# One decoder layer in fp32 on one core: merged rows kept on chip for a first operand, the gate's norm moved behind its product, final sums on VectorE, the last rows stored in two unequal parts

## The chip, the core and the metric

The kernel runs on one NeuronCore of a Trainium2 chip. The core has five engines, each with its own instruction queue that is worked off in order: TensorE (PE, matrix products into PSUM), VectorE (DVE, elementwise), ScalarE (ACT, elementwise with a function, a scale and a running sum), GpSimd (POOL) and SyncE (SP, which here issues all DMA transfers). Engines wait for each other through semaphores. The metric is the device time of one execution in microseconds (us); less is better. The time before is the median of three runs, 1106.02 us (1105.62 to 1108.62).

## The reference

One layer on x of shape (1024, 1024), all in fp32, cut to what matters here:

```python
h = rms_norm(x, norm_mix_g)
q, k, v, z_a, gk_low, cb, cc, xc, z_c, g_a, g_c = split(h @ w_in)
o = rms_norm(gla_chunked(q, k, v, gk), gla_norm_g)
y_a = (o * silu(z_a)) @ w_branch_a
y_c = ((cb * causal_dwconv(cc * xc, conv_w)) * silu(z_c)) @ w_branch_c
merged = sigmoid(g_a + b_ga) * y_a + sigmoid(g_c + b_gc) * y_c
x = x + merged @ w_out
ple_gate = sigmoid(rms_norm(x, norm_ple_g) @ w_ple_gate)
x = x + ple_gate * (p @ w_ple_proj)
return rms_norm(x, norm_final_g)

def rms_norm(x, g):
    return x * rsqrt(mean(x * x) + EPS) * g
```

The places of the change are `merged @ w_out`, the gate `rms_norm(x) @ w_ple_gate` and the last two lines.

## The kernel before

**Products.** Each fp32 product is made of three passes over a high and a low part of both operands (`mm3`; `split` makes the high part on ACT and the low part on DVE). A block product of 1024 x 1024 operands is made by a scheme with seven sub-products of 512 x 512 pieces in place of eight (`Cell.run`, products 0 to 6). An operand has four quadrants, loaded as raw tiles 0 to 3 (tag `raw`, eight buffers), and three to four sums of them: S1 = raw 1 + raw 3, S2 = S1 - raw 0, S3 and S4. A cell's products gather in three PSUM banks X, V and Y. Product 1 needs S1; V is copied or added out after product 1, and product 5 goes on in V. Cells run in pairs, their products alternating in the order 0, 1, 2, 3, 5, 4, 6. `run_groups` makes the operands (`prep`) up to seven products ahead and the loads up to thirteen.

**Stages.** Projections of h (`v`, `za`, `q`/`k`), the convolution branch (`conv`), gates, with the attention woven in (`att`), then the branch products `yc0..3` and `ya0..3`, the output projection `out0..3`, and the gate `gt0..3`. Of the last two, cell p holds the row blocks 2p and 2p + 1 (128 rows each). `merge_a` adds the two branches into a tile `ga`, which goes to the DRAM array `md`; `out` cells load their raw tiles from `md`.

**Around the output projection.** `make_out` loads two row blocks of x of 128 x 1024 into tiles of the pool `late`, which takes the place of the pool `sw`. The product is added onto them; the left halves by `cons`, the right halves straight from the banks Y and V by `onto`. A squared sum of each half gives the norm factor r (`rstd_of`, two POOL operations, the second a power of -0.5). `flip` scales the rows by r on ACT, turns them by PE transposes of 128 x 128 and multiplies them by the gain `gple` on DVE into tiles `gr` (three buffers), which go to the DRAM array `gd`, from where `gt` cells load. The rows themselves go to the DRAM array `x2d` once both halves are added.

**Around the end.** `make_gate` gives sigmoid on ACT, two DVE operations (times the projected embedding `pe`, plus x), a square with a sum on ACT, and the closing norm. The row blocks i = 1 of cells 2 and 3 are closed in pieces (`piece`): a block's pieces each add a sum (`pre`, `rf`; POOL), and the last piece makes the factor. Cell 3's last product is made in two halves of 256 columns, so that block has three pieces: columns 512 to 1023, 0 to 255, 256 to 511.

**Order.** The program is noted first and put in order by a planner (`Flow`): each operation has a cost, a latency and a due time counted back from the end; `put_in_order` lets the engine that can start first start the most urgent operation that is ready by then. PE's products keep the program's order; transposes (`side`) go where they fit. Buffers of a tag are given out in the order in which the program uses them first, so a tile that waits for a buffer holds back later tiles of its tag. `weave` spreads a generator's steps over the products: the weights of `w_out` and `w_ple_gate` (w = 0 and 1) are combined in the conv phase by `weights`, from tiles `wt` in place, and go to the DRAM arrays `wtd`; `bq` names the arrays that a stage loads.

All noted operations are issued by one line (491 in the profile), so groups are told apart by the names of their tiles.

Of the kernel before, what the change touches and what calls it, by code (L numbers as in the profile page):

```python
# [16 lines left out]
P = 128  # L17
# [229 lines left out]
class Flow:  # L247
# [12 lines left out]
    def note(self, engine, op, call, args, kw):  # L260
# [14 lines left out]
        o.lat = 0.15  # L275
        if engine == PE:
# [226 lines left out]
def kernel(  # L503
# [70 lines left out]
    gd = [[dram(f"gd{p}_{q}", 2, 4, P) for q in range(2)] for p in range(4)]  # L574
    wtd = [[dram(f"wtd{w}_{n}", 4, 512) for n in range(4)] for w in range(2)]

# [85 lines left out]

    def ring_steps(name, side, raw):

# [16 lines left out]
        if side == "A":  # L681
            a11, a21, a12, a22 = (r(n) for n in range(4))
            return [lambda: put(a11()), lambda: two("S1", a21, a22, ALU.add), lambda: two("S2", k("S1"), a11),
                    lambda: put(a12()), lambda: two("S3", a11, a21), lambda: two("S4", a12, k("S2"), over="S2"),
                    lambda: put(a22())]
# [9 lines left out]
    class Cell:  # L695


        def __init__(self, name, side, src, res, cons, prods=ORDER, begin=None, s1=None, u2=None, s5=None):
# [5 lines left out]
            self.steps = ring_steps(name, side, self.raw)  # L704

        def load(self, k):
            for n in NEED[self.side][k]:
                if self.raw[n] is None:
                    self.raw[n] = bp.tile([P, 4, P], F32, tag="raw", name=f"{self.name}raw{n}", bufs=8)
                    load(self.raw[n], self.src[n])  # L710
# [114 lines left out]

    def rstd_of(ms, name, ms2=None, tag="rstd"):
        r = sm.tile([P, 1], F32, tag=tag, name=name, bufs=4)
        if ms2 is None:
# [116 lines left out]

    merged = set()

    def merge_a(c, pool):
        def cons(i, j, src):
# [26 lines left out]
    nc.side = False  # L976
    for n in range(9):
        mm(warm[n % 6], zero[:, 0:P], zero, start=True, stop=True)
# [546 lines left out]
    def bq(w):  # L1525
        return [wb[w, 0], wtd[w][0], wtd[w][1], wb[w, 3], wtd[w][2], wb[w, 2], wtd[w][3]]

# [13 lines left out]
    for p in range(4):  # L1541
        outs.append(Cell(f"out{p}", "A", [md[p // 2][:, p % 2, n // 2, n % 2] for n in range(4)], wres, None))
    for c in outs[:2]:
# [5 lines left out]
    with phase("late", [ph["sw"], ep]) as lp:  # L1549
        flipped = set()  # L1550

        def make_out(p, cell):
# [3 lines left out]
            def begin():  # L1556
                for i in range(2):
                    xt.append(lp.tile([P, D], F32, tag="x", name=f"x2_{p}_{i}", bufs=4))
                    load(xt[i], x[rows(2 * p + i), :])
                    ms.append(sm.tile([P, 2], F32, tag="ms2", name=f"ms2_{p}_{i}", bufs=4))  # L1560

            def flip(i, r):
                act(xt[i], xt[i], AF.Copy, scale=r[:, 0:1])
                yield 4
                for qq in range(2):
                    pt = pso.tile([P, 4, P], F32, tag="o", name=f"pt_g{p}_{i}_{qq}", bufs=2)
                    for k in range(4):
                        kk = 4 * qq + k
                        transpose(pt[:, k, :], xt[i][:, kk * P:(kk + 1) * P])
                    g = lp.tile([P, 4, P], F32, tag="gr", name=f"gr{p}_{i}_{qq}", bufs=3)  # L1570
                    tt(g, pt, gple[:, 4 * qq:4 * qq + 4, None].to_broadcast([P, 4, P]), op=ALU.mult)
                    store(gd[p][qq][:, i], g)
                    yield 1
                flipped.add((p, i))

            def finish(i, j):
                js = slice(j * 512, (j + 1) * 512)
                act(junk[:, 0:512], xt[i][:, js], AF.Square, scale=1.0 / 32.0, accum_out=ms[i][:, j:j + 1])
                seen[i] += 1
                if seen[i] == 2:  # L1580
                    store(x2d[2 * p + i], xt[i])
                    r = rstd_of(ms[i][:, 0:1], f"rg{p}_{i}", ms[i][:, 1:2], tag="rg")
                    weave(flip(i, r), 4)

            def onto(i):
                def add(src):
                    tt(xt[i][:, 512:], src, xt[i][:, 512:], op=ALU.add)
                    return xt[i][:, 512:]
                return add

            def cons(i, j, src):
                if j == 0:
                    tt(xt[i][:, 0:512], src, xt[i][:, 0:512], op=ALU.add)
                finish(i, j)
# [7 lines left out]
        for p, c in enumerate(gts):  # L1602
            c.ready = lambda k, p=p: {(p, 0), (p, 1)} <= flipped
        with phase("sw4", lp.instead, lp) as pool:
# [4 lines left out]
        with phase("fin", [ph["sw4"]], lp) as gp:  # L1609
# [3 lines left out]
            def make_gate(p, cell):  # L1613
# [5 lines left out]
                def piece(i, cs, src, n, done):  # L1619
# [26 lines left out]
                    if a:  # L1646
                        nc.vector.tensor_scalar(xt[i][:, 0:a], xt[i][:, 0:a], r[:, 0:1], None, op0=ALU.mult)
                    store(out[rows(2 * p + i), 0:512], xt[i][:, 0:512])
# [15 lines left out]
                def cons(i, j, src):  # L1664
# [6 lines left out]
                    load(t, ped[2 * p + i][:, js])  # L1671
                    act(src, src, AF.Sigmoid)
                    tt(t, src, t, op=ALU.mult)
# [82 lines left out]
```

## Time and profile before

| What | us |
|---|---|
| median of three runs | 1106.02 |
| runs, lowest to highest | 1105.62 to 1108.62 |
| the profiled execution | 1105.2 |
| its span, first to last instruction | 1103.1 |
| PE busy | 1090.3 |
| DVE busy | 864.9 |
| ACT busy | 588.2 |
| POOL busy | 60.9 |

The profile is of one execution, whose time is 2.1 us over its span. Rows of a timeline give start, duration, engine, line, operation, output <- inputs and shapes; a bracket tells how long the engine was idle ahead of it and who ended that. Matmuls are pipelined: each is shown with some 0.39 us, while neighbours of 512 columns start 0.23 us apart, so a short stall shows in the starts and not in the busy time. `SPq` rows are DMA issues, and their duration is that of the issue, not of the transfer. Rows that group instructions give the count, then busy time and mean ns. Rows of stretches give the stretch and its length, then busy time and count of PE, weight loads, DVE, ACT and POOL, the granted PE clock, the share of the DMA engines and GB/s.

### The profile page before, as it was taken

How to read it: one execution, taken by the hardware profiler on the slowest of the kernel's cores; microseconds unless marked ns; L12 is line 12 of the kernel's file. 1: busy time of each engine (PE TensorE's matmuls, PEld its weight loads, DVE VectorE, ACT ScalarE, POOL GpSimd, SP SyncE). 2: the span in 40 equal slices, each digit the busy share in tenths (PEclk: the TensorE clock that was granted, in tenths of full speed). 3: DMA queues.
4: the chain of work that ended last, by engine and by line, in shares of the span. 5: the costliest groups of instructions: out<-in, count | busy, mean ns of one | idle time of the engine just before them, and what ended most of it. 6: DMA issues, size and time to landing. Idle time of an engine off the chain costs nothing. (4 is left out here: it accounts for less than half of the span.)

```text
span 1103.1 us, 15242 instructions
## 1 busy us (share of the span) xinstructions
PE 1090.3 (99%) x5049; PEld 907.2 (82%) x5049; DVE 864.9 (78%) x1391; ACT 588.2 (53%) x1083; POOL 60.9 (6%) x121
## 2 busy tenths in 40 slices
PE   9999999999999999999999999999999999999996
PEld 7888888788888888888888888888888887788885
DVE  6996477889878887748649687776999879879676
ACT  6775347866543433343334376765736344558554
POOL 0000000000000000000000022220000000102022
PEclk9999999999999999999999999999999999999998
DMA  9957463358777582212212699987694878788853
GB/s 317 326 188 241 135 211 106 115 186 249 243 228 259 170 290 99 89 58 67 86 63 74 224 302 350 324 259 278 237 306 158 307 260 296 273 271 297 293 182 133
DMA packets 149118, 235.79 MB, mean 214 GB/s; under 512 B 12592, under 2 KB 66096, under 8 KB 145968
## 3 DMA queue, kind: packets, MB, share of 16 engines
q1 hardware_dynamic: 149040, 234.83, 63.5%
q8 instruction: 39, 0.64, 0.2%
q14 instruction: 39, 0.32, 0.1%
HBM read 157.19 MB, written 77.59 MB: 213 GB/s over the span
## 5 line engine op out<-in xcount | busy, mean ns | idle before, releaser
L491 ACT ACTIVATE junk<-x 128x512 bf16<-128x512 f32 (+1 forms) x33 | 20.3, 617 | 20.4 <-DVE x L491 20.0
L491 ACT ACT_TABLE_LOAD x17 | 21.8, 1283 | 3.4 <-issue 2.4
L491 POOL MEMSET t<- 128x2 f32 x8 | 0.8, 99 | 378.4 <-DVE u L491 194.8
L491 DVE TENSOR_TENSOR wt<-wt 128x512 f32<-128x512 f32 x32 | 21.4, 684 | 0.2
L491 POOL TENSOR_TENSOR or<-or,mhalf 128x1 f32<-128x1 f32 x32 | 20.4, 639 | 2.7
L491 POOL TENSOR_SCALAR rg<-ms 128x1 f32<-128x1 f32 x8 | 5.9, 736 | 265.4 <-ACT junk L491 265.4
L491 DVE SCALAR_TENSOR_TENSOR u<-t,vec,u 128x1024 f32<-128x1024 f32 x16 | 20.4, 1276 | 0.0
L491 DVE COPY_PREDICATED aT<-trim,X 128x128 f32<-128x128 int32 x32 | 9.7, 302 | 13.3 <-PE X L491 12.7
L491 ACT ACTIVATE og<-op,or 128x256 f32<-128x256 f32 x32 | 15.1, 472 | 9.0 <-POOL or L491 7.4
L491 ACT CAST aTh<-aT 128x128 fp32r<-128x128 f32 x32 | 9.5, 298 | 11.3 <-DVE aT L491 9.9
L491 POOL TENSOR_SCALAR or<-oms 128x1 f32<-128x1 f32 x32 | 8.8, 275 | 118.9 <-ACT junk L491 118.9
L491 PE MATMUL op<-vl,aTh 128*128 128x256 f32 x64 | 15.0, 316 | 0.0
L491 PE MATMUL op<-Sh,qkl 128*128 128x256 f32 x56 | 14.5, 281 | 0.0
L491 DVE TENSOR_TENSOR gr<-pt_g,vec 128x512 f32<-128x512 f32 x16 | 10.7, 685 | 4.4 <-PE pt_g L491 3.6
L491 DVE TENSOR_TENSOR oT<-op,szl 128x256 f32<-128x256 f32 x32 | 13.3, 420 | 0.8 <-DMA szl<-szd 0.6
L491 ACT ACTIVATE junk<-op 128x256 bf16<-128x256 f32 x32 | 12.3, 385 | 2.0 <-PE op L491 1.7
L491 DVE TENSOR_TENSOR Sl<-S,Sh 128x256 fp32r<-128x256 f32 x28 | 11.8, 421 | 1.4 <-ACT Sh L491 1.1
L491 PE MATMUL pe<-wpehi,pThi 128*128 128x512 f32 x32 | 12.8, 399 | 0.0
L491 PE MATMUL pe<-wpehi,pTlo 128*128 128x512 f32 x32 | 12.7, 397 | 0.0
L491 PE MATMUL pe<-wpelo,pThi 128*128 128x512 f32 x32 | 12.6, 393 | 0.0
L491 PEld LDWEIGHTS X<-vl,keh 128*128 128x128 f32 x56 | 10.5, 188 | 2.3
L491 PE MATMUL X<-qkl 128*128 128x128 f32 x64 | 12.3, 274 | 0.0
(3231 smaller groups left out, 4158.1 us busy)
## 6 DMA issues: line engine op xcount, KB each, us to landing
qkl<-qkd SPq DMA_DIRECT2D x32, 320.0 KB, 4.8
wt<-in_wb_dram SPq DMA_DIRECT2D x8, 1024.0 KB, 6.4
wtd<-wt SPq DMA_DIRECT2D x32, 256.0 KB, 3.5
vl<-vd SPq DMA_DIRECT2D x32, 256.0 KB, 4.7
vraw<-in_wb_dram SPq DMA_DIRECT2D x28, 256.0 KB, 4.2
uq<-ud SPq DMA_DIRECT2D x5, 1024.0 KB, 6.4
oq<-od SPq DMA_DIRECT2D x5, 1024.0 KB, 6.0
hq<-in_xT_dram SPq DMA_DIRECT2D x8, 512.0 KB, 8.0
```

The source lines that it names most:

```text
L491: o.call(*[place(a) for a in o.args], **{k: place(a) for k, a in o.kw.items()})
```

## The change

- **Merged rows on chip.** For the row half i = 0 and the column blocks 4 to 7, `merge_a` writes the sum into a tile of the tag `raw` (`late`, named m4 to m7). It is still stored to `md`. `out0` and `out1` form S1 from raw tile 1 and these tiles, in four additions of 128 x 128 (`fresh`); raw tile 3 is loaded later, for product 6.
- **The norm in the gate's sigmoid.** The gain `gple` is multiplied into the weights of `w_ple_gate` on ACT in `weights` (16 operations of 128 x 512), and the three scaled quadrants go to three more arrays of `wtd` (12 stores). The rows are turned unscaled, half by half as soon as a half is added; a copy on ACT takes them out of PSUM. The factor r comes in as the scale of the gate's sigmoid (`rgate`).
- **x by halves.** For cells 0 and 1 the right halves of x are loaded into buffers of the tags `u2` and `s5`; `x2d` is stored by halves.
- **Sums by DVE.** The small additions of `piece` move from POOL to DVE; the power stays on POOL.
- **The last rows.** The closing scale of the last block is split into columns 640 to 1023 (ACT, stored by a DMA that ACT issues) and 0 to 639 (DVE, stored through SP); the last piece's product with the closing gain becomes an operation of its own ahead of the factor. For the block i = 1 of cell 2 the right half's scale moves from DVE to ACT.
- **Warm-up.** Ten matmuls in place of nine at the start; the planner knows a cost for a DMA issued by ACT.

```diff
@@ ring_steps
+            def s1():
+                if not fresh:
+                    return two("S1", a21, a22, ALU.add)
+                t = keep["S1"] = bp.tile([P, 4, P], F32, tag="T", name=f"{name}S1", bufs=4)
+                for kt in range(4):
+                    tt(t[:, kt, :], a21()[:, kt, :], fresh[kt](), op=ALU.add)
+                return put(t)
@@ merge_a
-            tt(g, g, m, op=ALU.add)
+            if i == 0 and k >= 4:
+                t = late[k - 4] = bp.tile([P, 512], F32, tag="raw", name=f"m{k}", bufs=8)
+                tt(t, g, m, op=ALU.add)
+                g = t
+            else:
+                tt(g, g, m, op=ALU.add)
@@
-    for n in range(9):
+    for n in range(10):
         mm(warm[n % 6], zero[:, 0:P], zero, start=True, stop=True)
@@ weights
+                    if w:
+                        for n, q in enumerate((b11, b12, b22, b21)):
+                            k = kt + 4 * (n >= 2)
+                            act(q, q, AF.Copy, scale=gple[:, k:k + 1])
+                            if n != 1:
+                                store(wtd[w][4 + (n + 1) // 2][:, kt, :], q)
@@ make_out
+                    t = lp.tile([P, D], F32, tag="x", name=f"x2_{p}_{i}", bufs=4)
+                    xt.append([t[:, 0:512], t[:, 512:]])
+                    if p < 2:
+                        xt[i][1] = bp.tile([P, 512], F32, tag=("u2", "s5")[i], name=f"x2r{p}_{i}", bufs=2)
...
-            def flip(i, r):
-                act(xt[i], xt[i], AF.Copy, scale=r[:, 0:1])
...
-                    tt(g, pt, gple[:, 4 * qq:4 * qq + 4, None].to_broadcast([P, 4, P]), op=ALU.mult)
+            def flip(i, j):
...
+                nc.scalar.copy(g, pt)
@@ finish
+                store(x2d[2 * p + i][:, j * 512:(j + 1) * 512], xt[i][j])
+                weave(flip(i, j), 2)
...
-                    store(x2d[2 * p + i], xt[i])
-                    r = rstd_of(ms[i][:, 0:1], f"rg{p}_{i}", ms[i][:, 1:2], tag="rg")
-                    weave(flip(i, r), 4)
+                    rgate[p, i] = rstd_of(ms[i][:, 0:1], f"rg{p}_{i}", ms[i][:, 1:2], tag="rg", bufs=8)
@@ piece
-                    act(src, src, AF.Sigmoid)
+                    act(src, src, AF.Sigmoid, scale=rgate[p, i][:, 0:1])
...
+                    if a or not done:
+                        tt(xc, xc, gf[:, cs], op=ALU.mult)
                     if not done:
-                        tt(xc, xc, gf[:, cs], op=ALU.mult)
...
-                        nc.gpsimd.tensor_scalar(pre, m, EPS if n == 0 else sums[i][:, 0:1], None, op0=ALU.add)
+                        nc.vector.tensor_scalar(pre, m, EPS if n == 0 else sums[i][:, 0:1], None, op0=ALU.add)
...
-                    nc.gpsimd.tensor_scalar(r, m, sums[i][:, 0:1], None, op0=ALU.add)
+                    nc.vector.tensor_scalar(r, m, sums[i][:, 0:1], None, op0=ALU.add)
                     nc.gpsimd.tensor_tensor(r, r, mhalf, op=ALU.pow)
                     if a:
-                        act(xt[i][:, 512:], xt[i][:, 512:], AF.Copy, scale=r[:, 0:1])
-                    else:
-                        nc.vector.tensor_scalar(xt[i][:, 512:], xt[i][:, 512:], r[:, 0:1], None, op0=ALU.mult)
+                        part = xt[i][:, 640:]
+                        act(part, part, AF.Copy, scale=r[:, 0:1])
+                        nc.scalar.dma_start(out[rows(2 * p + i), 640:], part)
+                        part = xt[i][:, 0:640]
+                        nc.vector.tensor_scalar(part, part, r[:, 0:1], None, op0=ALU.mult)
+                        store(out[rows(2 * p + i), 0:640], part)
+                        return
+                    act(xt[i][:, 512:], xt[i][:, 512:], AF.Copy, scale=r[:, 0:1])
```

More of the change, by code (lines that the diff above doesn't have):

```diff
@@ L275, in note @@
         o.lat = 0.15
-        if engine == PE:
+        if engine == ACT and op == "dma_start":
+            o.cost, o.lat = 0.1, 3.0
+        elif engine == PE:
             o.cost, o.lat = n / 2400 + 0.0134, 0.22
@@ L574 @@
     gd = [[dram(f"gd{p}_{q}", 2, 4, P) for q in range(2)] for p in range(4)]
-    wtd = [[dram(f"wtd{w}_{n}", 4, 512) for n in range(4)] for w in range(2)]
+    wtd = [[dram(f"wtd{w}_{n}", 4, 512) for n in range(4 + 3 * w)] for w in range(2)]
     load = nc.sync.dma_start
@@ L661, with ring_steps @@
             "B": ((0,), (0, 1), (2,), (3,), (2, 1), (2,), (3,))}
-    def ring_steps(name, side, raw):
+    def ring_steps(name, side, raw, fresh):
         keep = {}
@@ L682, in ring_steps @@
             a11, a21, a12, a22 = (r(n) for n in range(4))
-            return [lambda: put(a11()), lambda: two("S1", a21, a22, ALU.add), lambda: two("S2", k("S1"), a11),
+            def s1():
[5 more added lines that the diff above has]
+                return put(t)
+            return [lambda: put(a11()), s1, lambda: two("S2", k("S1"), a11),
                     lambda: put(a12()), lambda: two("S3", a11, a21), lambda: two("S4", a12, k("S2"), over="S2"),
@@ L703, in __init__ @@
             self.raw, self.ring = [None] * 4, {}
-            self.steps = ring_steps(name, side, self.raw)
+            self.steps, self.fresh = ring_steps(name, side, self.raw, fresh), fresh
         def load(self, k):
             for n in NEED[self.side][k]:
-                if self.raw[n] is None:
+                if self.raw[n] is None and not (self.fresh and k == 1 and n == 3):
                     self.raw[n] = bp.tile([P, 4, P], F32, tag="raw", name=f"{self.name}raw{n}", bufs=8)
@@ L824, in ev, with rstd_of @@
         return ep.tile([P, 512], F32, tag="ev", name=name, bufs=3)
-    def rstd_of(ms, name, ms2=None, tag="rstd"):
-        r = sm.tile([P, 1], F32, tag=tag, name=name, bufs=4)
+    def rstd_of(ms, name, ms2=None, tag="rstd", bufs=4):
+        r = sm.tile([P, 1], F32, tag=tag, name=name, bufs=bufs)
         if ms2 is None:
@@ L944, in merge_c @@
         return cons
-    merged = set()
+    merged, late = set(), {}
     def merge_a(c, pool):
@@ L1541 @@
     for p in range(4):
-        outs.append(Cell(f"out{p}", "A", [md[p // 2][:, p % 2, n // 2, n % 2] for n in range(4)], wres, None))
+        outs.append(Cell(f"out{p}", "A", [md[p // 2][:, p % 2, n // 2, n % 2] for n in range(4)], wres, None, fresh=[
+            lambda kt=kt, p=p: late[kt][:, (2 * p + 1) * P:(2 * p + 2) * P] for kt in range(4)] if p < 2 else ()))
     for c in outs[:2]:
@@ L1549 @@
     with phase("late", [ph["sw"], ep]) as lp:
-        flipped = set()
+        flipped, rgate = set(), {}
         def make_out(p, cell):
@@ new lines, in begin @@
+                    xt.append([t[:, 0:512], t[:, 512:]])
+                    if p < 2:
+                        xt[i][1] = bp.tile([P, 512], F32, tag=("u2", "s5")[i], name=f"x2r{p}_{i}", bufs=2)
+                        for j in (1, 0):
+                            load(xt[i][j], x[rows(2 * p + i), j * 512:(j + 1) * 512])
+                    else:
+                        load(t, x[rows(2 * p + i), :])
+                    ms.append(sm.tile([P, 2], F32, tag="ms2", name=f"ms2_{p}_{i}", bufs=4))
@@ L1576, in finish @@
+            def flip(i, j):
+                pt = pso.tile([P, 4, P], F32, tag="o", name=f"pt_g{p}_{i}_{j}", bufs=2)
+                for k in range(4):
+                    transpose(pt[:, k, :], xt[i][j][:, k * P:(k + 1) * P])
+                g = lp.tile([P, 4, P], F32, tag="gr", name=f"gr{p}_{i}_{j}", bufs=3)
+                nc.scalar.copy(g, pt)
+                store(gd[p][j][:, i], g)
+                yield 1
+                flipped.add((p, i, j))
             def finish(i, j):
-                js = slice(j * 512, (j + 1) * 512)
@@ L1578, in finish @@
-                act(junk[:, 0:512], xt[i][:, js], AF.Square, scale=1.0 / 32.0, accum_out=ms[i][:, j:j + 1])
+                store(x2d[2 * p + i][:, j * 512:(j + 1) * 512], xt[i][j])
+                weave(flip(i, j), 2)
+                act(junk[:, 0:512], xt[i][j], AF.Square, scale=1.0 / 32.0, accum_out=ms[i][:, j:j + 1])
                 seen[i] += 1
                 if seen[i] == 2:
-                    store(x2d[2 * p + i], xt[i])
-                    r = rstd_of(ms[i][:, 0:1], f"rg{p}_{i}", ms[i][:, 1:2], tag="rg")
-                    weave(flip(i, r), 4)
+                    rgate[p, i] = rstd_of(ms[i][:, 0:1], f"rg{p}_{i}", ms[i][:, 1:2], tag="rg", bufs=8)
@@ L1585, in onto @@
             def onto(i):
                 def add(src):
-                    tt(xt[i][:, 512:], src, xt[i][:, 512:], op=ALU.add)
-                    return xt[i][:, 512:]
+                    tt(xt[i][1], src, xt[i][1], op=ALU.add)
+                    return xt[i][1]
                 return add
@@ L1592, in cons @@
                 if j == 0:
-                    tt(xt[i][:, 0:512], src, xt[i][:, 0:512], op=ALU.add)
+                    tt(xt[i][0], src, xt[i][0], op=ALU.add)
                 finish(i, j)
@@ L1602 @@
         for p, c in enumerate(gts):
-            c.ready = lambda k, p=p: {(p, 0), (p, 1)} <= flipped
+            c.ready = lambda k, p=p: {(p, i, j) for i in range(2) for j in range(2)} <= flipped
         with phase("sw4", lp.instead, lp) as pool:
@@ L1671, in cons @@
                     load(t, ped[2 * p + i][:, js])
-                    act(src, src, AF.Sigmoid)
+                    act(src, src, AF.Sigmoid, scale=rgate[p, i][:, 0:1])
                     tt(t, src, t, op=ALU.mult)
```

19 lines of the change are left out of this document (3 added, 16 removed).

## The prediction

> **What bounds the kernel now.** I read the profile's page first (busy times), then the busy time by stretches, then TensorE's own timeline, gap by gap, and last the timeline of all engines over the end.
>
> ```profile
> span 1103.1 us, 15242 instructions
> PE 1090.3 (99%) x5049; PEld 907.2 (82%) x5049; DVE 864.9 (78%) x1391; ACT 588.2 (53%) x1083; POOL 60.9 (6%) x121
> ...
> 1095.00:1103.10 8.10, 0.00 (x0) 0.00 (x0) 3.19 (x8) 1.74 (x5) 3.00 (x5) 0.62 0.34 129
> ```
>
> TensorE (PE) is busy for 1090.3 of 1103.1 us, so an edit on another engine is worth only what it takes out of PE's few stalls or out of the stretch behind PE's last product: from 1095 on PE does nothing (second column after the length). The diff adds one warm-up matmul and takes none away. The stalls are found where starts of neighbouring matmuls lie further apart than the usual 0.23 us:
>
> ```profile
> 935.65 0.39 PE L491 MATMUL out1X<-wo0hi,out1lo 128*128 128x512 f32 x1
> 936.77 0.50 PE L491 MATMUL out0V<-wo1hi,out0hi 128*128 128x512 f32 x1 [0.73 <-ACT out0hi L491]
> 937.10 0.40 PE L491 MATMUL out0V<-wo1lo,out0hi 128*128 128x512 f32 x1
> 937.50 0.50 PE L491 MATMUL out0V<-wo1hi,out0lo 128*128 128x512 f32 x1
> 937.84 0.40 PE L491 MATMUL out0V<-wo1hi,out0hi 128*128 128x512 f32 x1
> ...
> 940.11 0.39 PE L491 MATMUL out1V<-wo1lo,out1hi 128*128 128x512 f32 x1
> 940.50 0.50 PE L491 MATMUL out1V<-wo1hi,out1lo 128*128 128x512 f32 x1
> ...
> 953.56 0.39 PE L491 MATMUL out1X<-wo3hi,out1lo 128*128 128x512 f32 x1
> 954.37 0.47 PE L491 MATMUL out0V<-wo5hi,out0hi 128*128 128x512 f32 x1 [0.42 <-DVE x L491]
> ...
> 956.97 0.39 PE L491 MATMUL out0V<-wo5hi,out0lo 128*128 128x512 f32 x1
> 957.56 0.47 PE L491 MATMUL out1V<-wo5hi,out1hi 128*128 128x512 f32 x1 [0.21 <-DVE x L491]
> ```
>
> All lie where the output projection begins. Beyond 0.23 the steps lose 0.89, 0.10, 0.17 and 0.11 (936.77 to 937.84), 0.16 (940.50), 0.58 (954.37) and 0.36 (957.56): 2.4 us. The bracket names the waits: the second product of `out0` waits for ScalarE's (ACT) cast of S1, the fifth products for VectorE's (DVE) additions onto the rows of x. Their history:
>
> ```profile
> 923.81 0.59 SPq L491 DMA_DIRECT2D md<-ga  x1
> ...
> 929.56 0.61 SPq L491 DMA_DIRECT2D out0raw<-md  x1
> ...
> 935.32 0.69 DVE L491 TENSOR_TENSOR out0S<-out0raw,out0raw 128x512 f32<-128x512 f32 x1
> ...
> 945.66 2.07 SPq L491 DMA_DIRECT2D x<-in_x_dram  x4
> ...
> 953.54 0.68 DVE L491 TENSOR_TENSOR x<-out0V,x 128x512 f32<-128x512 f32 x1
> ```
>
> The last merged rows go to DRAM (923.81) and come back by a load queued at 929.56; S1 is added at 935.32, the moment that PE runs out. The rows of x are asked for at 945.66 only, 16 us behind the first of these loads, since their tiles lie in a pool that replaces another.
>
> **Out projection, the part that gives time.** S1 of `out0` and `out1` now reads the merged rows where DVE wrote them. The store stays, but nothing of S1 waits for it. What still has to be loaded for S1 is raw tile 1, older rows of `md`; its buffer comes, in the buffers' order, behind the four merged tiles, the last of which is written just ahead of the 923.81 store. From the load to its use the old path took 935.32 - 929.56 = 5.8 us; counted from 923.8 that gives 929.6, so S1 comes some 5.7 us earlier, well beyond the 1.12 us step at 936.77. S1 costs DVE more, four additions of 128x128 for one of 128x512:
>
> ```profile
> L491 DVE TENSOR_TENSOR aTl<-aT,aTh 128x128 fp32r<-128x128 f32 x32 | 9.2, 288 | 0.8 <-ACT aTh L491 0.7
> L491 DVE TENSOR_TENSOR dds<-dcs x8: 149/156/157, 253.7 to 300.6; 128x4 f32<-128x4 f32 x8
> L491 ACT ACTIVATE x<-x,rg 128x1024 f32<-128x1024 f32 x8 | 9.2, 1145 | 0.0
> L491 DVE TENSOR_TENSOR gr<-pt_g,vec 128x512 f32<-128x512 f32 x16 | 10.7, 685 | 4.4 <-PE pt_g L491 3.6
> 380.00:420.00 40.00, 40.00 (x178) 33.14 (x177) 29.81 (x47) 14.94 (x26) 0.00 (x0) 1.00 0.82 289
> ```
>
> 4 x 0.288 - 0.69 = 0.46 us each, 0.9 for both, inside the 5.7 won; without that lead it would add to the first wait. The right halves of x move into the u2 and s5 buffers, which the branch products leave some 15 us ahead of 945.66, so both fifth-product waits should go. Value 2.4. The bounds are 0.94 (only the x waits go) and 2.4.
>
> **Edits that I cost at nothing, and their cover.** In the conv phase ACT gets 16 scalings of 128x512 and SP 12 stores of 256 KB. At half of the 1.145 us row for twice the width, some 0.6 us each, that is 10 us of ACT in a stretch (the row of 380 to 420) where ACT worked 14.9 of 40 us and PE all 40. The first subtraction in place now waits for its store to have read the block, and behind it on DVE stand the low parts of PE's coming weights; these are made up to seven products ahead, 7 x 12 x 0.23 = 19 us. Without that cover a late store would show on PE in full. In the out phase ACT loses eight scalings of 1.145 us (9.2) and gets sixteen evacuations of 128x512, at 0.6 about as much; DVE loses the sixteen `gr` products, 10.7 us. The `x2d` stores become sixteen halves, queued on SP earlier than now; what stands behind them is loads of gate weights, which have the same lead.
>
> At the start the tenth warm-up matmul delays the first real one by a step:
>
> ```profile
> 5.00 0.69 DVE L491 TENSOR_TENSOR pTlo<-pTraw,pThi 128x512 fp32r<-128x512 f32 x1
> ...
> 5.75 0.50 PE L491 MATMUL pe<-wpehi,pTlo 128*128 128x512 f32 x1
> ```
>
> The third real matmul waits for `pTlo`, ready at 5.69, whichever way the two ahead of it stand: 0, at worst 0.23.
>
> **The end.** The last rows' chain, with the operations that share the engines:
>
> ```profile
> 1095.00 0.28 POOL L491 TENSOR_SCALAR rf<-msl,pre 128x1 f32<-128x1 f32 x1 [1.52 <-ACT junk L491]
> ...
> 1095.20 0.75 DVE L491 TENSOR_TENSOR x<-x,pe 128x256 f32<-128x256 f32 x2
> ...
> 1096.32 0.80 POOL L491 TENSOR_SCALAR pre<-msl,pre 128x1 f32<-128x1 f32 x1 [0.28 <-ACT junk L491]
> ...
> 1096.62 0.19 ACT L491 ACTIVATION_READ_ACCUMULATOR junk<-x 128x1 f32 x1
> 1097.00 0.74 DVE L491 SCALAR_TENSOR_TENSOR x<-x,rf,gfin 128x512 f32<-128x512 f32 x1
> 1097.20 0.68 POOL L491 TENSOR_SCALAR rf<-msl,pre 128x1 f32<-128x1 f32 x1
> 1097.97 0.57 POOL L491 TENSOR_TENSOR rf<-rf,mhalf 128x1 f32<-128x1 f32 x1
> 1098.57 0.72 ACT L491 ACTIVATE x<-x,rf 128x512 f32<-128x512 f32 x1 [1.76 <-POOL rf L491]
> ...
> 1098.97 0.35 DVE L491 TENSOR_SCALAR x<-x,rf 128x256 f32<-128x256 f32 x1
> ...
> 1099.32 0.81 SPq L491 DMA_DIRECT2D out_dram<-x  x2
> ...
> 1100.00:1101.00 1.00, 0.00 (x0) 0.00 (x0) 0.00 (x0) 0.00 (x0) 0.00 (x0) 0.50 0.88 338
> 1101.00:1102.00 1.00, 0.00 (x0) 0.00 (x0) 0.00 (x0) 0.00 (x0) 0.00 (x0) 0.50 0.49 186
> ```
>
> The last square is read out at 1096.81, but GpSimd (POOL) adds the sums until 1097.88 and the power ends at 1098.54. With both sums on DVE: 0.1 hand-over, one small operation of 0.156 (the `dds` row), 0.1, the power 0.57: 1097.74, 0.80 less. The closing scale took 0.77 (1098.55 to 1099.32). In parts of 384 on ACT and 640 on DVE it takes what 0.72 for 512 leaves at 384, between 0.54 (by width) and 0.72; I take 0.61: 0.16 less. Best case 0.96. Against it: the small operations of the two earlier pieces and of the third block's sum now stand on DVE ahead of the last additions, 3 x 0.156 = 0.47 at most; and DVE's remaining product for the third block (0.74) can hold the power up. I take one small operation and 0.1 of the second: 0.7 gained. The lower bound is -1.0: 0.96 - 0.47 - 0.74, and 0.72 more if ACT's scale of the third block goes ahead of the last squares.
>
> The second store's own queue I cost at nothing: the 512 KB of both stores (338 + 186 KB in the last two rows, at a share of 0.88) flow without a gap, so an earlier second issue only lengthens the line. If it did help, it would be by one issue, half of 0.81.
>
> Sum: 2.4 + 0.7 = 3.1 us. The profiled execution took 1105.2 us, 2.1 of it around its span; by itself it would become 1102.1. The runs shown are 1105.62, 1106.02 and 1108.62; the profiled one and the lower two have the mean 1105.6, which I take as base: **1102.5**.
>
> **The rivals.**
> - *The power waits for DVE.* On POOL such an operation takes 0.28 (1095.00), but it has taken 2.04, ending just as a run of DVE additions over two SBUF tiles ended:
>
> ```profile
> 1003.86 2.35 DVE L491 TENSOR_TENSOR wg3lo<-wgq,wg3hi 128x1024 fp32r<-128x1024 f32 x2
> ...
> 1004.26 2.04 POOL L491 TENSOR_SCALAR rg<-ms 128x1 f32<-128x1 f32 x1 [0.71 <-ACT junk L491]
> ```
>
>   Now DVE stands idle during the power; after the change it has the last gain product and the 0.74 product to do just then. If both hold the power (0.37 + 0.74 = 1.1, of which 0.1 is in the sum), the 0.7 becomes -0.3: 1105.6 - 2.4 + 0.3 = 1103.5. For it: the 2.04. Against: the 0.74 may run while the squares are made. The Trainium skill has this rule ("SBUF — State Buffer", section "Who interferes with whom"): a DVE instruction with two SBUF inputs and a GpSimd instruction that reads SBUF share a port, and the later fully blocks. The 2.04 us row agrees.
> - *S1 stays late.* If the loads of raw tile 1 are queued no earlier than the old one, S1's wait stays and only the x waits go: 0.94 + 0.7 = 1.6, 1104.0. For it: four of the eight raw buffers are now held by merged rows. Against: nothing in these loads needs the last store.
> - *The second queue helps after all*: 0.4 more, 1102.1. Against it stands the full transfer share.
> - *Slower: ACT evacuates the turned rows.* ACT works in order, and `gr` has three buffers that wait for their stores; an evacuation that waits blocks the casts of PE's next weights behind it. A cast that is late costs what the first stall above cost, 1.27 us. It decides once the wait exceeds the lead of seven products; if it happens for half of sixteen, 8 x 1.27 - 3.1 = +7.1, 1112.7. Six such stalls (7.6) already give 1110.1. For it: ACT is on PE's path, where DVE's row of the same work shows waits of 4.4 in total. Against: that total hides in 19 us of lead, and ACT is the less busy engine (588 against 865 us).
>
> **How the numbers follow.** What a measurement of this kernel can tell from no change is about 0.3%, 3.3 us, so the line lies at 1102.7, just above my number. Forecast 0.60, with an own range of 1101.6 to 1103.4, of which 0.43 falls below the line; the second queue 0.07; the held power 0.11; S1 late 0.10; the slower one 0.12. Faster 0.50, same 0.17 + 0.11 + 0.10 = 0.38, slower 0.12. The range goes from 1101.0 (best end, second queue, all small stalls gone) to 1107.0, which takes in both rivals between and the lower end of the unknown costs (1105.6 - 0.94 + 1.0 = 1105.7), and leaves most of the slower case out.
>
> **What would show it.** Right: matmul steps of 0.23 from 935 to 958, S1 written in four parts near 930, x halves loaded ahead of 945; POOL with one power behind each sum, the last scale starting about 1 us behind the last square's read (1098.57 - 1096.81 = 1.76 now); the last two stores' transfer again some 1.4 us long. Wrong: new steps above 0.3 us anywhere in the out or gate products, above all with ACT named; a power longer than 0.7 us at the end; DVE waiting for raw loads near 930.

## The result, and the profile after

| | before | changed |
|---|---|---|
| median, us | 1107.23 (1105.62 to 1109.24, 6 runs) | 1102.97 (1102.36 to 1103.81, 6 runs) |
| the profiled execution, us | 1105.2 | 1103.81 |
| its span, us | 1103.1 | 1101.5 |
| start of the last matmul, us | 1093.01 | 1091.57 |
| from there to the end of the span, us | 10.09 | 9.93 |

The ratio is 0.9961, with a 95% interval of 0.9946 to 0.9976: the changed kernel is faster, by a small margin that is clear of no change. The forecast was 1102.5. The changed kernel run again beside new runs of the one before gave 1102.39 against 1106.14, a ratio of 0.9963 (0.9949 to 0.9977), and there its profiled execution had a span of 1100.5 and its last matmul at 1090.61, exactly the forecast 2.4 us ahead of 1093.01. So one profiled execution of the changed kernel is not like the next; what differs is told below.

First the page of the changed kernel (busy time, share, instructions) and the waits of its TensorE (total, count, longest):

```profile
span 1101.5 us, 15271 instructions
PE 1090.2 (99%) x5050; PEld 908.7 (83%) x5050; DVE 856.0 (78%) x1385; ACT 599.0 (54%) x1108; POOL 55.7 (5%) x116
...
PE warm L493 <- DVE zero L493: 1.4, 1, 1.4
```

PE's busy time is what it was, since the products are the same. Of its waits one is left, that of the first instruction of all; those for `out0hi` and for the rows of x are gone. The timeline of the output projection shows why (rows as before: start, duration, engine, output <- inputs):

```profile
922.55 0.44 SPq L493 DMA_DIRECT2D out0raw<-md  x1
...
924.46 1.40 SPq L493 DMA_DIRECT2D md<-m  x2
...
927.93 2.94 SPq L493 DMA_DIRECT2D x2r<-in_x_dram  x4
...
930.82 0.89 DVE L493 TENSOR_TENSOR out0S<-out0raw,m 128x128 f32<-128x128 f32 x4
...
936.38 0.39 PE L493 MATMUL out1X<-wo0hi,out1lo 128*128 128x512 f32 x1
936.61 0.39 PE L493 MATMUL out0V<-wo1hi,out0hi 128*128 128x512 f32 x1
936.83 0.39 PE L493 MATMUL out0V<-wo1lo,out0hi 128*128 128x512 f32 x1
...
939.10 0.39 PE L493 MATMUL out0V<-wo1hi,out0lo 128*128 128x512 f32 x1
939.33 0.39 PE L493 MATMUL out1V<-wo1hi,out1hi 128*128 128x512 f32 x1
```

Raw tile 1 is asked for at 922.55, ahead of the last stores of merged rows, and S1 is made in four parts from 930.82, 4.5 us earlier than the single addition at 935.32. The step into the second product is 0.23 (936.38 to 936.61), where it was 1.12.

The end of the same kernel, all engines:

```profile
1094.43 0.68 DVE L493 TENSOR_TENSOR x<-x,gfin 128x512 f32<-128x512 f32 x1
...
1094.59 1.72 POOL L493 TENSOR_TENSOR rf<-rf,mhalf 128x1 f32<-128x1 f32 x2 [7.85 <-DVE rf L493]
1094.80 0.19 ACT L493 ACTIVATION_READ_ACCUMULATOR junk<-x 128x1 f32 x1
1095.03 0.21 DVE L493 TENSOR_SCALAR rf<-msl,pre 128x1 f32<-128x1 f32 x1
1095.15 0.75 DVE L493 TENSOR_TENSOR x<-x,gfin 128x256 f32<-128x256 f32 x2
1095.55 1.41 ACT L493 ACTIVATE x<-x,rf 128x512 f32<-128x512 f32 x2 [0.56 <-POOL rf L493]
1095.82 0.74 DVE L493 SCALAR_TENSOR_TENSOR x<-x,rf,gfin 128x512 f32<-128x512 f32 x1
1096.30 1.31 SPq L493 DMA_DIRECT2D out_dram<-x  x3
1096.48 0.55 DVE L493 TENSOR_SCALAR x<-x,rf 128x640 f32<-128x640 f32 x1
1096.99 0.37 ACTq L493 DMA_DIRECT2D out_dram<-x  x1
```

The last square is read out at 1094.99 and the last scale ends at 1097.03: 2.04 us, against 2.51 before (1096.81 to 1099.32). But the two powers on POOL take 1.72 together, side by side with DVE's products of two SBUF tiles, where they took 0.67 and 0.57 before; and the four stores become ready within 0.8 us. What that does to the transfers is seen in the DMA share over the stretch from 1093 to 1103, in 40 slices of 0.25 us (tenths, 9 is 90% or more). Before:

```profile
DMA  0000000000000000000199999100399998000000
```

The changed kernel:

```profile
DMA  0000000000000000499999999995000000000030
```

Before, the bytes of the third closing block had been through for more than 0.5 us (two empty slices) when the last two stores began to flow. Now all four flow in one unbroken stretch of some 2.7 us: the last bytes wait for the first ones. From the moment at which the last rows are ready to the end of the span it takes 4.47 us in place of 3.78.

### The profile page after: what moved, and what is told of

It reads as the page before. It is cut to its first block, busy times and chain, and to the rows that moved or that the text cites. A ratio compares the mean times of both kernels' runs of the same rounds, so it can differ in the third digit from the quotient of the medians.

```text
span 1101.5 us, 15271 instructions
## 1 busy us (share of the span) xinstructions
PE 1090.2 (99%) x5050; PEld 908.7 (83%) x5050; DVE 856.0 (78%) x1385; ACT 599.0 (54%) x1108; POOL 55.7 (5%) x116
## 4 chain that ended last, share of the span: by engine, by line
PE 97%; DVE 1%; ACT 1%; issue 0%; POOL 0%; DVEq 0%; ACTq 0%
PE vacc L493 7%; PE op L493 3%; PE pe L493 2%; PE X L493 2%; PE ga3Y L493 1%; PE ga2Y L493 1%; PE ga1Y L493 1%; PE ga0Y L493 1%; PE out1Y L493 1%; PE gc1Y L493 1%; PE out3Y L493 1%; PE gc0Y L493 1%; PE out0Y L493 1%; PE out2Y L493 1%; PE za0Y L493 1%; PE xc3Y L493 1%
## 5 line engine op out<-in xcount | busy, mean ns | idle before, releaser
L493 ACT ACTIVATE junk<-x 128x512 bf16<-128x512 f32 (+1 forms) x29 | 17.8, 615 | 11.5 <-DVE x L493 11.0
L493 PE MATMUL op<-ident,og 128*128 128x128 f32 x64 | 12.3, 273 | 0.0
```

The costliest lines, as they stand in the source:

```text
L493: o.call(*[place(a) for a in o.args], **{k: place(a) for k, a in o.kw.items()})
```

## The experiments

The main theory: nearly all of the gain is S1's way through DRAM; the x halves and the end give less. The rivals: the x halves or the norm bear a share of their own; or the end does.

**The change again.** The same kernel, without an edit.

> The changed kernel once more, for its spread beside the same runs of before. If the tenth warm-up matmul itself delays the start, the first real matmul stands again near 5.9 us (5.09 before); if it was chance of that execution (a late first load, a late rise of the clock), it can stand anywhere from 5.1 to 5.9, and the span moves with it by as much. In either case no matmul step over 0.5 us between 935 and 960, and the last stores' transfer about 3 us long.

Measured: 1102.39 (nine runs), ratio 0.9963; spans from 1100.5 to 1101.4, while 23 executions of the kernel before had spans from 1102.9 to 1109.7 with a median of 1104.0. The spread is smaller as well as the mean, and the profile that the forecast was made from (1103.1) lay near the low end of the old one. The first real matmul stands at 5.53, so the tenth warm-up does not fix it near 5.9.

**The output projection undone: S1 by DRAM and x in whole rows.**

```diff
-            if i == 0 and k >= 4:
+            if False:
...
-                    if p < 2:
+                    if False:
```

(and `fresh=()`)

> S1 again from the rows that come back from DRAM, and the right halves of x again in the pool that opens late; all else as changed. If the gain is the output projection's stalls (2.4 us in the prediction), this is 2.0 to 2.6 us slower than the changed kernel and PE's steps of 0.8 to 1.1 us near 936, 954 and 957 are back. If the tail gives the gain (0.7 or more) and the stalls were hidden anyway, it is within 0.5 us of the changed kernel.

Measured: 1104.47, ratio to before 0.9977 (0.9962 to 0.9991). That is 2.1 us over the change run again (1102.39), in the range expected if the projection gives the gain. PE again waits 0.9 us for `out0hi` (a step of 1.28), but no wait for x stands in this profile, where three large steps were expected.

**The old end.** `piece` as before: sums on POOL, scales and stores as they were.

> The closing of the last rows as before (sums on POOL, halves of 512, both stores through SP), all else as changed. Prediction: 0.7 us slower than the changed kernel, from the last matmul to the end of the span 9.8 us. Rival, read from the changed kernel's trace: the scale ends 0.85 us sooner but the four last stores then run into each other, so the two differ by 0.2 us or less.

Measured: 1102.92, ratio 0.9962 (0.9948 to 0.9976), as the whole change. From the last matmul to the end it took 9.93 us, to the hundredth what the new end took. The new end is worth nothing that these runs can tell: the median is 0.53 above that of the change run again, and the interval of either ratio is some 1.5 us to each side.

**Nine warm-up matmuls.** `for n in range(9)` in the changed kernel.

> Nine warm-up matmuls, all else as changed. If the tenth one costs what the trace of the changed kernel seems to show, the first real matmul stands near 5.1 us and the kernel is 0.4 to 0.8 us faster than with ten. If it was chance or the third matmul's data decide (prediction), no difference beyond 0.2 us.

Measured: 1102.67, ratio 0.9957 (0.9940 to 0.9974): no difference.

**S1 alone undone.** Only `if i == 0 and k >= 4` and `fresh` are taken back; x still comes by halves.

> Only S1 goes back to the rows from DRAM; the halves of x stay in their early buffers. If the DRAM round trip is what varies between executions, this kernel shows the slow outliers of the kernel before (spans from 1 to 4 us over its fastest), its fastest span is 1.3 to 1.6 us over the changed kernel's 1100.5 (the first product's step of about 1.1 us near 936 is back), and no step over 0.5 us near 953 to 957. If x's late loads vary, its spans lie within 1 us of each other.

Measured: 1105.82, ratio 0.9989 (0.9978 to 0.9999). All else together is worth about 0.1%. The ten spans go from 1102.6 to 1105.6, so they spread as expected, but the lowest is 2.1 over the changed kernel's 1100.5 and not 1.3 to 1.6. The profiled execution is the longest of the ten. In it PE (the idle time ahead of a row in brackets) stops for 2.43 us for the cast of S1, and something follows that had not been expected:

```profile
936.29 0.39 PE L493 MATMUL out1X<-wo0hi,out1lo 128*128 128x512 f32 x1
939.11 0.79 PE L493 MATMUL out0V<-wo1hi,out0hi 128*128 128x512 f32 x1 [2.43 <-ACT out0hi L493]
939.70 0.63 PE L493 MATMUL out0V<-wo1lo,out0hi 128*128 128x512 f32 x1
940.13 0.63 PE L493 MATMUL out0V<-wo1hi,out0lo 128*128 128x512 f32 x1
940.55 0.63 PE L493 MATMUL out0V<-wo1hi,out0hi 128*128 128x512 f32 x1
...
942.59 0.40 PE L493 MATMUL out0V<-wo1hi,out0lo 128*128 128x512 f32 x1
942.83 0.39 PE L493 MATMUL out0V<-wo1hi,out0hi 128*128 128x512 f32 x1
```

The same kernel's busy time by stretches, with the granted PE clock third from the right:

```profile
930.00:936.00 6.00, 6.00 (x28) 4.99 (x27) 4.33 (x6) 2.00 (x2) 0.00 (x0) 1.00 1.04 362
936.00:940.00 4.00, 1.57 (x6) 0.89 (x5) 2.61 (x5) 1.19 (x2) 0.00 (x0) 0.88 1.01 375
940.00:943.00 3.00, 3.00 (x9) 2.41 (x9) 3.00 (x6) 2.53 (x5) 0.00 (x0) 0.59 0.48 145
```

After the pause the matmuls go 0.59 and then 0.43 us apart, not 0.23, until 942.26, at a granted clock of 0.59 from 940 to 943. The step of 2.82 loses 2.59 and the eight after it (939.11 to 942.59) lose another 3.48 - 8 x 0.227 = 1.66: the pause costs 4.25 us in all. Before, a pause of 0.73 cost 1.27 with the uneven steps behind it, and the granted clock from 936 to 940 was 1.00. Four of the ten executions, those with spans of 1105.2 to 1105.6, have a mean granted clock of 0.996, the other six 0.997 or 0.998; so it seems that the half rate came in four of them.

**x in whole rows.** Only `if p < 2` is taken back.

> Only the right halves of x go back to the late pool; S1 stays on chip. If the two waits are independent, the steps near 953 and 957 are back (0.6 and 0.4 us) and its span is 0.7 to 1.1 us over the changed kernel's. If the x waits were only a result of S1's lateness, it is within 0.3 us of the changed kernel.

Measured: 1103.18, ratio 0.9961 (0.9946 to 0.9976), and PE has no wait for x. The rows of x are asked for at 943.40, and the fifth products find their banks added in time.

**The third block's sums on POOL, the last block's on DVE.** `(nc.gpsimd if p == 2 else nc.vector)` in both sums.

> The sums of the third block (cell 2) go back to POOL, the last block's stay on DVE. If the end is set by four stores that come ready together, the third block's factor and its stores come some 0.5 to 0.8 us sooner and the stretch from the last matmul to the end shrinks from 9.9 to about 9.4 us. If the last block's power on POOL alone sets it, 9.9 stays.

Measured: 1103.12, ratio 0.9965 (0.9953 to 0.9978); the last stretch took 9.90. ACT now scales the third block (1094.25, 0.72) ahead of the last square, which puts the last scale's end 0.65 later than in the changed kernel, while the stores do not meet. The one pays for the other.

**The norm undone.** The gain goes back to the turned rows and r to a copy on ACT ahead of the turn. The rows are still stored and turned in halves, but only once both halves are added.

```diff
-            def flip(i, j):
+            def flip(i, j, r):
+                act(xt[i][j], xt[i][j], AF.Copy, scale=r[:, 0:1])
+                yield 4
...
-                nc.scalar.copy(g, pt)
+                tt(g, pt, gple[:, 4 * j:4 * j + 4, None].to_broadcast([P, 4, P]), op=ALU.mult)
```

> The norm goes back into the rows (scaled by ACT, gain on DVE, factor not in the sigmoid), all else as changed. Prediction: this part costs and gives nothing, so the times agree within 0.3 us. Rival: ACT's evacuations and the folded gain cost stalls in the out or gate products; then this kernel is faster by as much, with the steps near 1016 and 1087 gone.

Measured: 1103.49 (four runs), ratio 0.9962 (0.9947 to 0.9977): no difference.

**S1 alone done.** The kernel before, with the merged rows on chip and nothing else.

> The kernel before with one part of the change alone: the merged rows of S1 reach the projection on chip, everything else as before. If S1's way through DRAM was nearly the whole gain, its spans lie within 0.5 us of the changed kernel's 1100.5 to 1101.4, without outliers, and the time is 1102.4 to 1103.2. If the other parts matter together, it is 0.5 to 1.0 us slower than the changed kernel (1103.3 or more).

Measured: 1104.20 (eleven runs), ratio 0.9975 (0.9966 to 0.9984), spans 1101.3 to 1103.7: the second branch of the expectation. Its PE does not wait for `out0hi`, but it does elsewhere:

```profile
PE warm L491 <- DVE zero L491: 1.4, 1, 1.4
PE out0V L491 <- ACT junk L491: 0.9, 1, 0.9
PE pt_g L491 <- ACT x L491: 0.7, 1, 0.7
PE out1V L491 <- DVE x L491: 0.2, 1, 0.2
```

The timeline says what stands behind them. ACT's `junk` in the second line only ended last; what frees the bank V is DVE's addition onto x (952.35), the third in a row that began with a wait for the load of x:

```profile
951.15 0.69 DVE L491 TENSOR_TENSOR x<-out0Y,x 128x512 f32<-128x512 f32 x1 [0.42 <-DMA x<-in_x_dram]
...
951.86 0.39 PE L491 MATMUL out1X<-wo3hi,out1lo 128*128 128x512 f32 x1
...
952.35 0.69 DVE L491 TENSOR_TENSOR x<-out0V,x 128x512 f32<-128x512 f32 x1
...
953.19 0.47 PE L491 MATMUL out0V<-wo5hi,out0hi 128*128 128x512 f32 x1 [0.94 <-ACT junk L491]
...
955.81 0.39 PE L491 MATMUL out0V<-wo5hi,out0lo 128*128 128x512 f32 x1
956.37 0.47 PE L491 MATMUL out1V<-wo5hi,out1hi 128*128 128x512 f32 x1 [0.17 <-DVE x L491]
...
1006.98 1.15 ACT L491 ACTIVATE x<-x,rg 128x1024 f32<-128x1024 f32 x1
...
1007.06 0.39 PE L491 MATMUL out2Y<-wo6hi,out2hi 128*128 128x512 f32 x1
...
1008.17 1.09 PE L491 MATMUL pt_g<-ident,x 128*128 128x128 f32 x8 [0.73 <-ACT x L491]
```

With S1 early, PE reaches the fifth product before the rows of x are added: the steps there are 1.33 and 0.56, where before had 0.81 and 0.59. And a turn of rows, still behind the norm, is now met by an earlier PE: a step of 1.11 at 1007.06. In this execution these 1.10 + 0.33 + 0.88 = 2.3 us beyond the usual steps give back what S1 won: its last matmul starts at 1093.01, as before.

**Both last stores by SyncE.** `store(out[rows(2 * p + i), 640:], part)` in place of `nc.scalar.dma_start`; one execution, as the next two.

> The changed kernel with both of the last two stores issued by SyncE. If what the 16 DMA engines move bounds the end, the tail from the last matmul's start to the span's end stays at 9.9 us (9.7 to 10.0). If the issue itself counts, the fourth store is issued some 0.4 us later and the tail is 10.2 to 10.4.

Measured: 1103.37; 9.87 us from the last matmul to the end, as expected if the bytes set it. ACT's own queue is worth nothing that this one execution shows.

**Half of the last bytes left out.** The two stores of the third closing block are taken away.

> The changed kernel without the stores of the third closing block (its 128 rows are computed and not stored), so that half of the bytes of the end are missing. If the stores that become ready together set the end, the tail shrinks from 9.9 us by 1.0 to 1.4. If the chain of squares, powers and scales sets it, by 0.3 at most.

Measured: 1103.20; 9.20 us from the last matmul to the end, 0.7 less than with all four stores. That lies between the two expectations. Its DMA share, again from 1093 to 1103:

```profile
DMA  0000000000000000004999990000000000000200
```

The last 512 KB come through alone, and the end follows 3.73 us behind the last scale, as before the change.

**All sums on POOL.** Both small additions of `piece` go back to `nc.gpsimd`; the rest of the new end stays.

> The changed kernel with all closing sums of squares on GpSimd again. If the stores' bytes bound the end, the last scale ends 0.4 to 0.9 us later and the tail stays within 0.2 us of 9.9. If the compute chain bounds it, the tail grows by 0.4 to 0.9, to 10.3 to 10.8.

Measured: 1101.79, the lowest of all times in this study, from a single execution; 9.69 us from the last matmul to the end. Its DMA share from 1093 to 1103:

```profile
DMA  0000000004999991999996000000000000000000
```

The sums on POOL make the chain slower by 0.4, but the third block is stored earlier, and the two pairs hardly meet. The slower chain did not lengthen the stretch to the end (10.3 to 10.8 was expected if the chain bounded it), which speaks for the stores. Whether this variant is faster than the changed kernel was not measured with an interval.

The ends side by side, all from profiled executions, in us:

| kernel | last matmul starts | last scale ends, after it | then to the end | sum |
|---|---|---|---|---|
| before | 1093.01 | 6.31 | 3.78 | 10.09 |
| S1 alone done | 1093.01 | 6.07 | 3.72 | 9.79 |
| old end | 1090.77 | 6.17 | 3.76 | 9.93 |
| third block's sums on POOL | 1090.90 | 6.11 | 3.79 | 9.90 |
| all sums on POOL | 1090.31 | 5.89 | 3.80 | 9.69 |
| third block not stored | 1091.30 | 5.47 | 3.73 | 9.20 |
| changed | 1091.57 | 5.46 | 4.47 | 9.93 |
| both stores by SyncE | 1091.43 | 5.72 | 4.15 | 9.87 |

The third column falls into two groups: 3.7 to 3.8 where the pairs of stores don't meet, 4.1 to 4.5 where they do. Five more profiles with the new end, of runs told of above, fall into the second group (4.10 to 4.55 in the third column). The three old ends differ by 0.3 among themselves in the last column, and with these five the new ones go from 9.47 to 10.01, so a gain of 0.1 or 0.2 in the last column is no finding.

## Why the prediction came out right, and where it did not

**The output projection, 2.4: right, for the reason given.** Every wait that it names is gone. Between the profiled executions of before and of the changed kernel's second measurement the last matmul moves by 2.40. Between 930 and 965 the steps beyond the usual ones add up to 2.7 before and to 0.1 there, and 0.2 of that gain is lost again at the products of the gate, by a step that is new and stands in both profiles of the changed kernel. In the first one:

```profile
1088.29 0.39 PE L493 MATMUL gt2Y<-wg6hi,gt2lo 128*128 128x512 f32 x1
1088.72 0.39 PE L493 MATMUL gt3Y<-wg6hi,gt3hi 128*128 128x256 f32 x1
```

In this first profile the last matmul moves by 1.44 only: that execution lost 0.65 at its start (below), and some 0.3 more than the second between 1005 and 1020, where rows are turned. S1's lead was 4.5 us and not 5.7: the load of raw tile 1 was asked for 7.0 us earlier, but took 7.7 to land, so that from load to use it was 8.3 and not 5.8.

What was missed is that one profile does not tell the price of the old path. In three profiles with it (before, the projection undone, S1 alone undone) the pause is 0.73, 0.89 and 2.43 us, and the last of these cost 4.25. Whether the long executions of the kernel before are of this kind was not seen in a profile of theirs, and their mean clock leaves it open: of 53 executions, 0.996 is read in four of the seven with spans of 1107.0 or more, and in four of the other 46. S1's path is not all that varies, either: with S1 alone done the spans still go from 1101.3 to 1103.7. The ratios agree on the size: S1 alone is worth 0.25%, all else without it 0.11%, the whole 0.37%, so the two add up, to 2.8, 1.2 and 4.1 us of 1107, and S1 alone gives some two thirds and not nearly all (the intervals, about 0.1% to either side, are wide for this sum, and the ratios come from different sets of runs).

**Within it, the x halves (0.94): right that the waits go, wrong that the halves are what takes them away.** They are also gone with x in whole rows, as long as the rest of the change stands. S1 alone leaves them and lengthens the first to a step of 1.33. So the x halves and the rows stored and turned by halves seem each to cover what the other leaves: undone one by one (x halves, norm, end, warm-up) nothing was lost that can be told, undone together about 1.3 us (0.9975 against 0.9963; the intervals still touch). Whole rows of x were asked for at 943.40 with the rest of the change and at 944.58 without; which part moves them was not separated. Nor was it settled whether the x halves, queued ahead of S1's loads, make a late S1 later: with S1 by DRAM the time was 1105.82 with the halves and 1104.47 without them, in different sets of runs whose intervals touch.

**The end, 0.7: mis-sized, and this is the step that failed.** It measured 0.16 between the two profiles and 0.00 between the changed kernel's first profile and that of the old end; the medians of these two kernels differ by 0.53, inside the intervals, so the runs by themselves do not exclude 0.7. The terms on the engines were fair: a sum on DVE took 0.21 (0.156 was used), the last scale ends 0.85 sooner after the last matmul. Wrong was to let the time from there to the end stand at 3.78. For the third block the forecast counted some time of DVE; what counts is that its factor comes later (its power ends 3.95 us after the last matmul, where it was 3.03), and so do its 512 KB, which then stand in the line ahead of the last 512. 0.85 - 0.69 = 0.16. That line is shown, by one execution and by the two groups of the table: without the third block's stores the end comes 3.73 behind the last scale and not 4.47.

**The rival of the held power was half right.** The two powers took 0.93 and 0.82, both over the 0.7 that the prediction names as a sign of being wrong: 1.72 together against 2 x 0.57, so 0.58 was lost, as the Trainium skill ("SBUF — State Buffer", section "Who interferes with whom") has it for DVE's instructions with two SBUF inputs. With all sums on POOL each power is back at 0.57. The end that it gave (0.3 lost) did not come: the last square was read out 3.42 after the last matmul and not 3.80, and this 0.38 is in the 0.85. The rival of S1 that stays late is out (922.55 against 929.56), and so is ACT as the new bound: no wait of PE for ACT.

**The second queue at nothing: right.** With SyncE alone the end is as long (9.87, one execution). The Trainium skill ("DMA: Bandwidth & Descriptors", section "Issuing engines are not separate DMA queues") says that all issuers share the same 16 engines and that a second one saves the issue only; the run agrees.

**The work in the conv phase at nothing: right.** PE has no wait there. DVE now waits 1.6 us in all for the stores of `wt`, and none of it reaches PE.

**The start at nothing: right on the count, wrong on the reason's reach.** Nine warm-ups in place of ten change nothing, but the start itself varies (below). One reading in the prediction is off, without effect: in the row of the stretch from 1095 on, PE's time is the first column behind the length, not the second.

**The base, 1105.6: too low by 0.5 to 1.6.** Four sets of runs of the kernel before have the medians 1107.23, 1106.14, 1107.12 and again 1107.12. Gain and base were both taken from the low end of the runs, and so the time, 1102.5, lies within 0.5 of 1102.97 and of 1102.39, while the gain between medians is 3.75 to 4.3 and not 3.1. That the time came out so close is in part luck: a base and a gain that are both too low cancel. Of the 3.75, 0.9 is what the median execution of the kernel before took beyond the profiled one (spans of 1104.0 and 1103.1), 0.4 lies outside the span (below), and some 2.5 are what the profiles show.

## What to carry to other kernels

One profile does not price a round trip through DRAM on the path of a busy TensorE: here the pause was 0.73, 0.89 and 2.43 us in three profiles, and the longest also slowed the products behind it. When a stall is removed, read which loads and which norm the faster engine will meet next, and mend those with it. At the end of a kernel, when the last rows are ready is half of the answer; the other half is whether the bytes of the rows ahead of them are through by then.

## What the hardware showed that was not expected

**Behind a pause of 2.4 us the products went at half rate for some 3 us**, shown above by the steps of 0.43 and the granted clock of 0.59. It is one pause, in the longest of ten executions. The trace's records of the granted clock, from which that column is made, have half speed from 939.05 to 942.46, for 3.41 us. In all fourteen profiles every such record but the last of a trace lasts a whole number of times 3.41 us (1, 46, 273, 319 or 320 times). So it counts where a pause lies, and not only how long it is: in the stretch of 3.41 us that ends at 939.05 PE was idle for 2.37. Behind the last matmul of each profile the clock fell at the end of the first such stretch in which PE was idle for 2.45 us or more, while stretches with up to 0.96 us of idle time left it full, the pauses of 0.73 and 0.89 us near 936 among them. What a stretch in between does, no run shows.

The Trainium skill ("TensorE: Matmul & The Clock Gate", section "Part 1: The HAM clock gate (the "warmup" mystery)") tells of a half rate after an idle window of about 3.4 us, in windows that run freely, and of a steady half-rate step of 426.7 ns for 512 columns. The step agrees, and 3.41 us agrees with the window; but the pause here was a microsecond shorter than that window, and it was enough.

**At the start products go at half rate too, and the granted clock's column doesn't show it.** The first products of the changed kernel's first profile:

```profile
5.87 0.63 PE L493 MATMUL pe<-wpehi,pThi 128*128 128x512 f32 x1
6.29 0.63 PE L493 MATMUL pe<-wpelo,pThi 128*128 128x512 f32 x1
6.72 0.63 PE L493 MATMUL pe<-wpehi,pTlo 128*128 128x512 f32 x1
7.15 0.49 PE L493 MATMUL pe<-wpehi,pThi 128*128 128x512 f32 x1
7.47 0.39 PE L493 MATMUL pe<-wpelo,pThi 128*128 128x512 f32 x1
```

Its stretch from 5.8 to 7.2, by the same columns as above:

```profile
5.80:7.20 1.40, 1.40 (x5) 1.05 (x4) 1.29 (x3) 1.08 (x2) 0.00 (x0) 1.00 0.96 329
```

Three steps of 0.43 at a granted clock that reads 1.00. That reading is empty: the trace's first record of the clock, at full speed, begins at 7.33 only, and time without a record counts as 1.00. In the second profile of the same kernel this record begins at 4.98, the first product starts at 5.53, and the steps behind it are 0.34, 0.38, 0.35 and then 0.24. In all fourteen profiles the matmuls, warm-ups included, step by 0.43 (the very first by 0.59) up to the first record, which begins between 4.56 and 7.33, and by less from there on. That is the 0.65 us by which the two profiles differ from the start on, and no edit stands behind it.

**The time around the span moves too.** The kernel before has a median of 2.2 us between its span and its time, the changed one 1.8, the kernel with S1 alone done 1.8 as well, and the others with several runs 1.8 to 2.0. This 0.4 us of the gain lies outside all that the trace shows; its cause stays open.
